# Attention scores with all products over 128 rows instead of 128 and 64 in turn

## The chip, the cores and the metric

The kernel runs on one core of one Trainium2 chip. The metric is the device time of one execution in microseconds (us); lower is better. Engines are named as the profile names them: PE is TensorE's matmul side, PEld its weight loads, DVE is VectorE, ACT is ScalarE, POOL is GpSimd, and SP is SyncE, which issues every DMA of this kernel.

## The reference, cut to what matters

Two transformer layers over 512 main tokens and 256 context tokens, width 1024. Layer 0 mixes a multi-scale pooling with grouped-query attention (12 query heads, 4 key heads, head size 64), layer 1 mixes a latent attention (8 heads of 64 + 32 = 96 dimensions) with a neighbourhood attention (8 heads of 64, each query against a window of 256 keys and 256 context keys). Each layer ends in a gated feed forward. Cut to the attention:

```
# layer 0: main tokens against 768 keys, context tokens against 256
s = einsum("bqhgd,bkhd->bhgqk", q, k) * 64 ** -0.5
o = einsum("bhgqk,bkhd->bqhgd", softmax(s), v)
# layer 1, latent heads, q and k of 96 dimensions: main tokens against 768 keys
# layer 1, neighbourhood heads
s_win = einsum("bqhd,bqkhd->bhqk", q_r, k_w) * scale + bias
s_ctx = einsum("bqhd,bchd->bhqc", q_r, k_ctx) * scale
p = softmax(concatenate([s_win, s_ctx]))
```

All of it is float32.

## The kernel before

Every float32 matrix is kept as two parts, H + L, each representable in the format fp32r that PE multiplies. An ordinary product (`mm3`, lines 134 to 138) is three matmuls: H with H, H with L and L with H.

For heads of 64 dimensions the parts of two heads, A and B, are stacked on the 128 partitions, so that two matmuls do. `stack_q` (line 345) writes QA = [A.H; A.L] and QB = [B.L; B.H]. `stack_k` (line 351) writes KA = [A.H; A.H], KB = [B.H; B.H] and KL = [A.L; B.L]; lines 356 and 357 are the two ACT copies that fill the second halves of KA and KB. A score block is then one product over 128 rows, Q with KA or KB, and one over 64 rows, the H half of Q with its half of KL (`hr = slice(64 * hd, 64 * hd + 64)`):

```
for ko in (MAIN, CTX):
    pe.matmul(S[:, ko], Q[:, tq], K[:, ko], start=True, stop=False)
    last = pe.matmul(S[:, ko], Q[hr, tq], KL[kp][hr, ko], start=False, stop=True)
```

The two kinds alternate in three places. Layer 0, main tokens (`main_units`, lines 767 and 768): 48 sets (6 pairs, 4 query tiles, 2 heads) of four products, of 512, 512, 256 and 256 keys. Layer 0, context tokens (`ctx_units`, lines 795 and 796): 12 sets of four products of 256. Layer 1, neighbourhood (`na_units`, lines 1057 and 1058): 16 units (4 pairs, 4 query blocks), each of two heads with four products of 256. The latent heads (`mla_units`) use `mm3` over 96 rows: 32 sets of six products, 512 three times and 256 three times, with no 64-row product among them.

All four loops run through `pipeline` (line 383). A unit is the scores and the softmax of one set: DVE takes the maximum (line 364), ACT the exponential (line 369), DVE a reciprocal (371), POOL the division (373). Two or three units later PE transposes the probabilities (line 380), ACT or DVE copies them out of PSUM (`copy_out`, lines 166 and 168), and PE multiplies them with the values (lines 746, 1026, 1206), each product with 64 columns of weights. Layer 0 also fits in steps of the modulation weights (line 206) whose loads come through the four buffers `wr`. Scores lie in two PSUM tiles `ps_big` or four `ps_one`.

The order of the instructions on each engine's queue, SP's too, is fixed when the program is built: a list scheduler walks the program in priority order on simulated times, so later work moves ahead where it is ready. Buffers come from pools; a tile waits until all readers of what lay in its place are done. The 12 slots `x3` (`slot3`) hold KA, KB and KL of the neighbourhood heads, later the latent keys; the slots `cH` and `cL` (8 each) hold the context's normalised input, later the biases. Before the neighbourhood loop six DMAs move halves of V into V2 (lines 1009, 1010), and each pair loads six bias tiles (1042), which POOL multiplies (1043). `turn_pair` (line 1096) transposes and splits latent queries and keys into rows 0 to 95 of their tiles. The tile `rows` (line 707) holds ten gain rows on all partitions for the whole run.

Of the kernel before, what the change touches and what calls it, by code (L numbers as in the profile page):

```python
# [26 lines left out]
# first 128-column tile of every 512-column block of layer 0's modulation weights, in the order of use  # L27
# [14 lines left out]
def trunk(ctx: ExitStack, tc: tile.TileContext, A: dict, out: bass.AP):  # L42
# [3 lines left out]
    # ------------------------------------------------------------------ pools  # L46
# [7 lines left out]
    def banks(i):  # L54
        """The 4 banks of PSUM that the next phase takes in pairs (ps_big) or one by one (ps_one)."""
        nonlocal ps
        psum.close()
        ps = psum.enter_context(tc.tile_pool(name=f"ps{i}", bufs=2, space=bass.MemoryType.PSUM))
# [19 lines left out]
    def group_pair(g, name):  # L78
        """H and L tiles for the main (g = 0: 512) or the context tokens (g = 1: 256)."""
        n, w = ((TM, "m"), (TC, "c"))[g]  # L80
        return tuple(base.tile([P, n], F32R, tag=w + x, name=name + x, bufs=KT) for x in "HL")
# [10 lines left out]
    # ---------------------------------------------------------------- loading  # L92
# [21 lines left out]

    def load(src, cols):
        raw = wrp.tile([P, 1024], F32, tag="wr", name="wraw")
        sp.dma_start(out=raw[:, :cols], in_=src)
        return raw

    def split(raw, cols, hp, tag="ws", bufs=3, eng=dve):  # L120
        """raw = H + L exactly, both representable in float32r."""
# [20 lines left out]
    def later(f, n=2):  # L142
        """Run f after the next n blocks of products have been issued."""
        waiting.append((blocks[0] + n, f))
        waiting.sort(key=lambda w: w[0])
# [6 lines left out]
    def run_chunks(chunks):  # L152
        """chunks: (load, compute(units)); loads run one chunk ahead."""
# [8 lines left out]
    def copy_out(dst, src, acts=1, of=2):  # L162
        """PSUM -> SBUF, `acts` of every `of` calls on the scalar engine."""
# [6 lines left out]
    # ------------------------------------------------------------ modulation  # L170
# [8 lines left out]
    def ada_quarter(qt, psum, ws, sbm, between=lambda: None):  # L179
        """shift and scale columns of feature tiles 2 qt, 2 qt + 1; ws: their weights [128, 512] per k tile"""  # L180
# [15 lines left out]
    def ada_steps(blocks, psum, slot):  # L196
        """Closures for column blocks (1024 wide) of layer 0's modulation: one per k tile, and a last one."""
# [54 lines left out]
    def square_sum(xs, sl, slot=lambda name: slot3(F32, name)):  # L252
        """sums of the squares over the k tiles"""
# [11 lines left out]
    def rstd_of(xs, sl, slot=lambda name: slot3(F32, name), between=lambda: None):  # L265
        """1 / rms of every token of the slice, on all partitions, in PSUM."""
# [29 lines left out]
    # ---------------------------------------------------------------- shared  # L296
    def tok_gemm(pt, units, kper, n, hs, ks=None):
        """pt [128 tokens, n] = h @ w over the k tiles (all, or ks of them); hs: per k (H, L) of the 128 tokens."""
# [5 lines left out]
    def tile_of(h, t):  # L304
        """per k (H, L) of token tile t (0-3 main, 4-5 context)."""
# [3 lines left out]
    def feature_gemm(pt, units, hs):  # L309
        """pt [128 features, tokens] over all k tiles; units: per k (WH, WL); hs: per k (H, L)."""  # L310
# [6 lines left out]
    def rope(dst, src, C, S, half, tmp):  # L317
        """dst = src * C + swap_halves(src) * S, over views [.., 2 * half]; the sum is left to later."""
# [5 lines left out]
    def head_rstd(view, sb, sqb=2):  # L324
        """1 / rms over the last axis of view [128, tiles, heads, d]; also the scratch tile for that."""
# [10 lines left out]
    def split_out(H, L, s, g=None):  # L336
        """PSUM s, times the column g if given -> H + L"""
# [7 lines left out]
    def stack_q(QA, QB, sl, s, g=None):  # L345
        """s [128: head A, head B] (times g) -> QA = [A.H; A.L], QB = [B.L; B.H] stacked on the partitions."""
# [4 lines left out]
    def stack_k(KA, KB, KL, sl, s, g=None):  # L351
        """KA = [A.H; A.H], KB = [B.H; B.H], KL = [A.L; B.L]."""
# [6 lines left out]
    # -------------------------------------------------------------- attention  # L359
    def softmax(S, nh, n, scale, pr, mx=None):  # L360
        """S [128 queries, nh heads, n keys] in PSUM -> normalised pr[head] [128, n] in SBUF."""
# [13 lines left out]
    def transposed(blocks, dst, acts=1, of=2):  # L375
        """128 x 128 blocks of probabilities -> dst [128 keys, len(blocks), 128 queries]."""
# [6 lines left out]
    def pipeline(units, fill, lag):  # L383
        """units: (scores + softmax, transposes) closures; fill: rates of background closures per step."""
# [26 lines left out]
    # ----------------------------------------------------------- feed forward  # L411
    def ffn(layer, xs, groups, chunks, last, background=None, grouped=None, ends=None, lead=1, pre=None, nbuf=(2, 1)):
        """Residual feed forward. groups: (token slice, condition, h); last(m) or, by the token groups `ends`, grouped(i).
        The first `lead` column tiles are taken group by group."""
        off, last_of = 0, []
        nmax = max(n for _, n in chunks)
        with ExitStack() as own:
# [4 lines left out]
            def ws_unit(src, cols):  # L422
                """weights, in turn in the buffers of the pool `pre` and of the one here"""
# [78 lines left out]
    def mix_out(layer, mixs, xs, groups, wp, after, ws):  # L502
        """groups: (token slice, condition, per k (H, L)); ws: the weights of the first output tiles."""
# [11 lines left out]
    # ================================================================ layer 0  # L515
# [32 lines left out]
    with tc.tile_pool(name="g0", bufs=1, side="left") as gp, tc.tile_pool(name="ws0", bufs=1, side="right") as wp:  # L548
# [5 lines left out]
        def pair_rows(kind, hv, t0, sink):  # L554
            """hv [128, token tiles from t0, 4 heads, 64]: RMS norm, rotation (main tokens), transposes: sink(pair, tokens, psum)."""
# [87 lines left out]
        # queries: pair p holds heads p (rows 0-63) and p + 6 (rows 64-127)  # L643
# [10 lines left out]
        def to_k(pr, *a):  # L654
            stack_k(KA[pr], KB[pr], KL[pr], *a)

        def first_chunk(units):
            """keys and the first queries, over the k tiles in quarters as their modulation comes in"""
# [48 lines left out]
        rows = base.tile([P, A["rows"].shape[1]], F32, tag="rows", name="rows")  # L707
        sp.dma_start(out=rows, in_=A["rows"].partition_broadcast(P))
        grow = {k: rows[:, a:b] for k, (a, b) in ROWCOLS.items()}
        # rotary tables with the head gains folded in  # L710
# [10 lines left out]
        KL = [kvp.tile([P, TT], F32R, tag=f"KL{i}", name=f"KL{i}") for i in range(2)]  # L721
# [10 lines left out]
    with tc.tile_pool(name="at0", bufs=1, side="left") as ap:  # L732
        pvq = []
        adaq = [f for b in (2, 4) for f in ada_steps([b, b + 1], ps_pv, lambda: m_slot("L", "adat"))]

        def pv_steps(p, t, last, k0, pts, st, m):
            """values of query tile t of a pair, two key tiles a step"""
# [15 lines left out]
        def main_units(p):  # L753
            pvs = {}
            kp = p // 3
            for t in range(4):
                pts = []
                for hd in range(2):
                    tq = slice(128 * t, 128 * t + 128)
                    hr = slice(64 * hd, 64 * hd + 64)  # L760
                    Q, K = (QA, QB)[hd][p], (KA, KB)[hd][kp]
                    st = {}

                    def scores(Q=Q, K=K, tq=tq, hr=hr, hd=hd, st=st):
                        S = ps_big([P, 1024])
                        for ko in (MAIN, CTX):
                            pe.matmul(S[:, ko], Q[:, tq], K[:, ko], start=True, stop=False)  # L767
                            last = pe.matmul(S[:, ko], Q[hr, tq], KL[kp][hr, ko], start=False, stop=True)  # L768
# [14 lines left out]
        def ctx_units(p):  # L783
            pvs = {}
            kp = p // 3
            for t in range(2):
# [3 lines left out]
                def scores(tq=tq, st=st):  # L790
                    S = ps_big([P, 2, 512])
                    for hd in range(2):
                        hr = slice(64 * hd, 64 * hd + 64)
                        Q, K = (QA, QB)[hd][p], (KA, KB)[hd][kp]
                        pe.matmul(S[:, hd, :TC], Q[:, tq], K[:, CTX], start=True, stop=False)
                        last = pe.matmul(S[:, hd, :TC], Q[hr, tq], KL[kp][hr, CTX], start=False, stop=True)
# [46 lines left out]
    class Ada1:  # L843
        """Layer 1's modulation goes along with layer 0's feed forward, on the vector engine."""
# [44 lines left out]
    # ================================================================ layer 1  # L889
# [534 lines left out]
```

## Time and profile before

| | |
|---|---|
| time, median of 3 runs | 1822.68 us (1812.99 to 1824.0) |
| span of the profiled execution | 1820.5 us, first to last instruction |
| what lies around the span | not listed apart; the median lies 2.2 us above it |
| PE busy | 1766.2 us (97%) |
| DVE, ACT, POOL busy | 947.5, 648.6, 234.4 us |
| mean granted TensorE clock | 0.978 |

PE's busy time is a union of modelled instruction spans, which overlap: the next matmul starts well before the one before it is shown to end. What a product costs is therefore read from start to start in the timeline, not from its shown length. The granted clock is 1.0 at 2.4 GHz and 0.5 at 1.2 GHz.

### The profile page before, as it was taken

The numbers are of one execution on the slowest core, as the hardware profiler recorded it, in microseconds if no ns is written. First come the engines' busy times: TensorE is split into PE (matmuls) and PEld (weight loads), VectorE is DVE, ScalarE is ACT, GpSimd is POOL, SyncE is SP. The second block draws the span as 40 slices with busy tenths as digits, with TensorE's granted clock in tenths as the row PEclk, the third lists the DMA queues.
The fourth block names the chain that finished last, engine by engine and source line by source line (L and its number), as shares of the span: only waits on it lengthen the run. The fifth ranks groups of instructions, "written<-read, shape, count | busy, mean of one in ns | idle before, by whom it ended". The sixth has DMA issues, their size and how long they took to land.

```text
span 1820.5 us, 28940 instructions
## 1 busy us (share of the span) xinstructions
PE 1766.2 (97%) x11590; PEld 1505.8 (83%) x11590; DVE 947.5 (52%) x2080; ACT 648.6 (36%) x1269; POOL 234.4 (13%) x360
## 2 busy tenths in 40 slices
PE   6899999999999999999999999998899999999999
PEld 3697556679888888888889999667778999899897
DVE  5686445545774533532336884446855543333332
ACT  4454334534321221121123563344455343232231
POOL 1342222301000000000000202323321000000000
PEclk9998999999999999999999999789999999999999
DMA  8310213421353532531222221102001222232221
GB/s 300 125 47 34 93 71 115 163 93 47 108 173 129 176 104 88 177 101 58 70 70 73 82 74 58 52 8 79 24 24 63 78 94 93 96 96 96 95 79 61
DMA packets 57638, 166.90 MB, mean 92 GB/s; under 512 B 6560, under 2 KB 13472, under 8 KB 57504
## 3 DMA queue, kind: packets, MB, share of 16 engines
q1 hardware_dynamic: 57504, 165.06, 27.3%
q8 instruction: 91, 1.49, 0.3%
q14 instruction: 43, 0.35, 0.1%
HBM read 160.05 MB, written 4.19 MB: 90 GB/s over the span
## 4 chain that ended last, share of the span: by engine, by line
PE 92%; DVE 4%; ACT 2%; DMA 1%; issue 1%; SPq 0%; POOL 0%; ACTq 0%; DVEq 0%; POOLq 0%
PE ps_one L137 16%; PE ps_one L138 16%; PE ps_one L136 16%; PE ps_tp L380 5%; PE ps_tp L138 5%; PE ps_tp L136 5%; PE ps_tp L137 5%; PE ps_pv L746 3%; PE ps_pv L1206 2%; PE ps_big L768 2%; PE ps_big L136 2%; PE ps_pv L1026 2%; PE ps_big L767 2%; PE ps_big L137 2%; PE ps_big L138 2%; PE ps_pv L136 1%
## 5 line engine op out<-in xcount | busy, mean ns | idle before, releaser
L124 ACT CAST wH<-wraw 128x1024 fp32r<-128x1024 f32 (+5 forms) x209 | 194.2, 937 | 382.9 <-PE ps_one L137 199.4
L125 DVE TENSOR_TENSOR wL<-wraw,wH 128x1024 fp32r<-128x1024 f32 (+4 forms) x199 | 222.5, 1122 | 171.2 <-ACT wH L124 168.7
L137 PE MATMUL ps_one<-hL,wH 128*128 128x512 f32 (+1 forms) x704 | 236.8, 336 | 0.0
L138 PE MATMUL ps_one<-hH,wL 128*128 128x512 f32 (+1 forms) x704 | 236.8, 336 | 0.0
L136 PE MATMUL ps_one<-hH,wH 128*128 128x512 f32 (+1 forms) x704 | 236.7, 336 | 0.0
L138 PE MATMUL ps_tp<-hH,wL 128*128 128x256 f32 x704 | 196.6, 280 | 0.0
L137 PE MATMUL ps_tp<-hL,wH 128*128 128x256 f32 x704 | 196.3, 279 | 0.0
L136 PE MATMUL ps_tp<-hH,wH 128*128 128x256 f32 x704 | 196.0, 280 | 0.0
L138 PE MATMUL ps_one<-aH,wL 128*128 128x512 f32 (+1 forms) x560 | 194.0, 347 | 0.0
L137 PE MATMUL ps_one<-aL,wH 128*128 128x512 f32 (+1 forms) x560 | 193.9, 347 | 0.0
L136 PE MATMUL ps_one<-aH,wH 128*128 128x512 f32 (+1 forms) x560 | 193.5, 347 | 0.0
L138 PEld LDWEIGHTS ps_one<-hH,wL 128*128 128x128 f32 x704 | 132.2, 188 | 15.4
L137 PEld LDWEIGHTS ps_one<-hL,wH 128*128 128x128 f32 x704 | 132.2, 188 | 14.5
L136 PEld LDWEIGHTS ps_one<-hH,wH 128*128 128x128 f32 x704 | 132.3, 188 | 14.1
L373 POOL TENSOR_SCALAR prob<-prob,rs 128x768 f32<-128x768 f32 (+2 forms) x136 | 106.0, 782 | 291.6 <-DVE rs L371 124.2
L290 POOL TENSOR_SCALAR hH<-nt 128x256 fp32r<-128x256 f32 (+1 forms) x72 | 39.5, 557 | 739.4 <-ACT nt L289 737.6
L136 PEld LDWEIGHTS ps_tp<-hH,wH 128*128 128x128 f32 x704 | 132.3, 188 | 0.9
L137 PEld LDWEIGHTS ps_tp<-hL,wH 128*128 128x128 f32 x704 | 132.0, 188 | 1.0
L138 PEld LDWEIGHTS ps_tp<-hH,wL 128*128 128x128 f32 x704 | 132.3, 188 | 0.1
L364 DVE TENSOR_REDUCE mx<-ps_big 128x1 f32<-128x768 f32 (+1 forms) x92 | 84.8, 922 | 90.9 <-PE ps_big L768 59.8
L136 PEld LDWEIGHTS ps_one<-aH,wH 128*128 128x128 f32 x560 | 105.8, 189 | 14.7
L137 PEld LDWEIGHTS ps_one<-aL,wH 128*128 128x128 f32 x560 | 105.6, 189 | 14.5
(297 smaller groups left out, 3623.1 us busy)
## 6 DMA issues: line engine op xcount, KB each, us to landing
wraw<-in_ada_dram SPq DMA_DIRECT2D x80, 512.0 KB, 3.9
wraw<-in_wg_dram SPq DMA_DIRECT2D x44, 512.0 KB, 3.5
wraw<-in_wu_dram SPq DMA_DIRECT2D x44, 512.0 KB, 3.5
wraw<-in_wd_dram SPq DMA_DIRECT2D x32, 384.0 KB, 3.1
wraw<-in_wd_dram SPq DMA_DIRECT2D x16, 512.0 KB, 3.5
wraw<-in_w1n_dram SPq DMA_DIRECT2D x12, 512.0 KB, 3.5
adaw<-in_adaq_dram SPq DMA_DIRECT2D x16, 256.0 KB, 5.4
wraw<-in_adaq_dram SPq DMA_DIRECT2D x8, 512.0 KB, 4.9
```

Source lines behind the costliest of these rows:

```text
L124: act.copy(H, raw[:, :cols])
L125: eng.tensor_tensor(L, raw[:, :cols], H.bitcast(F32), op=ALU.subtract)
L136: pe.matmul(o, aH, bH, start=first, stop=False)
L137: pe.matmul(o, aH, bL, start=False, stop=False)
L138: return pe.matmul(o, aL, bH, start=False, stop=last)
L290: last = (pool.tensor_scalar(H, t[:, :n], 1.0, 1.0, op0=ALU.mult, op1=ALU.mult), sub(L, t[:, :n], H))
L364: dve.reduce_max(mx[:, :nh], S, axis=AX)
L373: pool.tensor_scalar(pr[i], pr[i], r[:, i:i + 1], 1.0, op0=ALU.mult, op1=ALU.mult)
L380: pe.transpose(tp[:, 128 * i:128 * i + 128], b, ident)
L746: pe.matmul(st["pv"][64 * hd:64 * hd + 64, tq], V[kt][:, 64 * kv:64 * kv + 64], pts[hd][:, kt - k0, :], start=kt == k0, stop=kt == 5)
L767: pe.matmul(S[:, ko], Q[:, tq], K[:, ko], start=True, stop=False)
L768: last = pe.matmul(S[:, ko], Q[hr, tq], KL[kp][hr, ko], start=False, stop=True)
```

## The change

Layer 0: the low parts of the keys go into LA = [A.L; B.L] (the old KL). At the start of the attention a new function copies each half to both halves by DMA, so that LA = [A.L; A.L] and LB = [B.L; B.L], and the second product becomes Q, all 128 rows, with LA or LB. (It now also adds low times low.) This is done for both key pairs, for main and context columns apart: 12 DMAs. LB takes a new tile of the attention's pool and a slot `cH`.

Layer 1, neighbourhood: the roles turn round. Keys are stacked [A.H; A.L] and [B.L; B.H] by `stack_q` (no KL, no ACT copies), queries are split whole into QQ = (H, L), each [A; B], and at the start of each pair the same function copies halves: 6 DMAs a pair, 24 in all, into tiles with two buffers per part. V2 moves to three of the slots `x3` that KL held.

Latent heads: POOL sets rows 96 to 127 of each query and key tile to zero in `turn_pair` (80 memsets of 32 x 256), and the products run over 128 rows.

The tile `rows` is replaced by two loads of parts of it, four rows for layer 0 and, at the start of layer 1, six for layer 1. All else in the diff is comments taken out.

```diff
+    def gain_rows(hp, names):
+        at, end = ROWCOLS[names[0]][0], ROWCOLS[names[-1]][1]
+        rows = hp.tile([P, end - at], F32, tag="rows", name="rows")
+        sp.dma_start(out=rows, in_=A["rows"][:, at:end].partition_broadcast(P))
+        return {k: rows[:, ROWCOLS[k][0] - at:ROWCOLS[k][1] - at] for k in names}
...
+    def both_halves(XA, XB):
+        a, b = (x.bitcast(F32) for x in (XA, XB))
+        for hr in (slice(0, 64), slice(64, 128)):
+            sp.dma_start(out=b[hr], in_=a[64:128])
+        sp.dma_start(out=a[64:128], in_=a[0:64])
...
-            stack_k(KA[pr], KB[pr], KL[pr], *a)
+            stack_k(KA[pr], KB[pr], LA[pr], *a)
...
     with tc.tile_pool(name="at0", bufs=1, side="left") as ap:
+        LB = []
+        for a in LA:
+            LB.append((ap.tile([P, TM], F32R, tag="LB", name="LBm", bufs=2),
+                       base.tile([P, TC], F32R, tag="cH", name="LBc", bufs=KT)))
+            for b, ko in zip(LB[-1], GROUPS):
+                both_halves(a[:, ko], b)
+        LA = [tuple(a[:, ko] for ko in GROUPS) for a in LA]
...
-                    hr = slice(64 * hd, 64 * hd + 64)
-                    Q, K = (QA, QB)[hd][p], (KA, KB)[hd][kp]
+                    Q, K, L = (QA, QB)[hd][p], (KA, KB)[hd][kp], (LA, LB)[hd][kp]
...
-                        for ko in (MAIN, CTX):
+                        for g, ko in enumerate(GROUPS):
                             pe.matmul(S[:, ko], Q[:, tq], K[:, ko], start=True, stop=False)
-                            last = pe.matmul(S[:, ko], Q[hr, tq], KL[kp][hr, ko], start=False, stop=True)
+                            last = pe.matmul(S[:, ko], Q[:, tq], L[g], start=False, stop=True)
...
-                        last = pe.matmul(S[:, hd, :TC], Q[hr, tq], KL[kp][hr, CTX], start=False, stop=True)
+                        last = pe.matmul(S[:, hd, :TC], Q[:, tq], L[1], start=False, stop=True)
...
+    grow = gain_rows(lp, ("mqr", "mqrp", "mkr", "mkrp", "qag", "kvag"))
...
+    QQ = [[nap.tile([P, TM], F32R, tag=f"nQ{x}{i}", name=f"nQ{x}{i}") for x in "HL"] for i in range(4)]
...
-    KL = [slot3(F32R, name="nKL") for _ in range(4)]
...
-        to_q = lambda pr, *a: stack_q(QA[pr], QB[pr], *a)
-        to_k = lambda pr, *a: stack_k(KA[pr], KB[pr], KL[pr], *a)
+        to_q = lambda pr, sl, *a: split_out(QQ[pr][0][:, sl], QQ[pr][1][:, sl], *a)
+        to_k = lambda pr, *a: stack_q(KA[pr], KB[pr], *a)
...
-        V2 = [ap.tile([P, 512], F32, tag=f"V2{i}", name=f"V2{i}") for i in range(3)]
+        V2 = [slot3(F32, name=f"V2{i}")[:, :512] for i in range(3)]
...
+            QB = [ap.tile([P, TM], F32R, tag="nQB" + x, name="nQB" + x, bufs=2) for x in "HL"]
+            for a, b in zip(QQ[pr], QB):
+                both_halves(a, b)
...
-                            pe.matmul(S[:, so], Q[:, tq], K[:, ko], start=True, stop=False)
-                            last = pe.matmul(S[:, so], Q[hr, tq], KL[pr][hr, ko], start=False, stop=True)
+                            pe.matmul(S[:, so], QH[:, tq], K[:, ko], start=True, stop=False)
+                            last = pe.matmul(S[:, so], QL[:, tq], K[:, ko], start=False, stop=True)
...
+            for x in dst[2 * h2 + a]:
+                pool.memset(x[96:128, sl].bitcast(F32), 0.0)
...
-                            last = mm3(S[:, ko], (QH[:96, tq], QL[:96, tq]), (KH[:96, ko], KL_[:96, ko]), True, True)
+                            last = mm3(S[:, ko], (QH[:, tq], QL[:, tq]), (KH[:, ko], KL_[:, ko]), True, True)
```

## Rows read from the trace of the kernel before

**Rows 1.** The chain that ended last, shares of the span by engine.

```profile
PE 92%; DVE 4%; ACT 2%; DMA 1%; issue 1%; SPq 0%; POOL 0%; ACTq 0%; DVEq 0%; POOLq 0%
```

**Rows 2.** Stretches: length, each engine's busy us (instructions), clock, DMA share, GB/s.

```profile
188.50:334.90 146.40, 146.10 (x991) 88.35 (x990) 71.89 (x176) 60.24 (x130) 36.23 (x40) 1.00 0.27 98
1149.30:1168.10 18.80, 18.76 (x58) 12.50 (x58) 7.90 (x34) 7.07 (x19) 6.03 (x10) 0.50 0.11 32
1168.10:1212.50 44.40, 44.40 (x269) 30.14 (x270) 24.57 (x96) 19.98 (x50) 14.71 (x23) 1.00 0.07 20
1212.50:1229.50 17.00, 17.00 (x84) 12.12 (x82) 6.23 (x30) 6.53 (x16) 3.82 (x6) 0.70 0.00 0
```

**Rows 3.** Timeline, layer 0's output projection: two plain 128-row products of 512 in a row.

```profile
400.40 0.39 PE L138 MATMUL ps_one<-mixH,wL 128*128 128x512 f32 x1
...
400.63 0.40 PE L136 MATMUL ps_one<-mixH,wH 128*128 128x512 f32 x1
```

**Rows 4.** Timeline, one layer-0 main set: start us, us, engine, line.

```profile
188.84 0.47 PE L767 MATMUL ps_big<-KA,QA 128*128 128x512 f32 x1
...
189.25 0.18 PEld L768 LDWEIGHTS ps_big<-KL,QA 64*128 64x128 f32 x1 [0.24 <-issue]
189.25 0.49 PE L768 MATMUL ps_big<-KL,QA 64*128 64x512 f32 x1
...
189.67 0.38 PE L767 MATMUL ps_big<-KA,QA 128*128 128x256 f32 x1
...
189.99 0.38 PE L768 MATMUL ps_big<-KL,QA 64*128 64x256 f32 x1
...
190.29 0.66 PE L746 MATMUL ps_pv<-PT,V 128*64 128x128 f32 x8
```

**Rows 5.** Timeline, one latent set of six products, behind transposes, then values.

```profile
1348.21 0.48 PE L136 MATMUL ps_big<-mKH,mQH 96*128 96x512 f32 x1
...
1348.29 0.19 PEld L137 LDWEIGHTS ps_big<-mKL,mQH 96*128 96x128 f32 x1
1348.53 0.39 PE L137 MATMUL ps_big<-mKL,mQH 96*128 96x512 f32 x1
...
1348.99 0.28 PE L136 MATMUL ps_big<-mKH,mQH 96*128 96x256 f32 x1
...
1349.22 0.28 PE L138 MATMUL ps_big<-mKH,mQL 96*128 96x256 f32 x1
...
1349.43 0.54 PE L1206 MATMUL ps_pv<-PT,mV 128*64 128x128 f32 x3
```

**Rows 6.** Timeline, one context set of layer 0: its start and what follows.

```profile
338.95 0.36 PE L795 MATMUL ps_big<-KA,QA 128*128 128x256 f32 x1
...
340.18 0.66 PE L746 MATMUL ps_pv<-PT,V 128*64 128x128 f32 x8
```

**Rows 7.** Timeline, neighbourhood: eight products in a row, then transposes.

```profile
1209.18 0.38 PE L1057 MATMUL ps_one<-nKA,nQA 128*128 128x256 f32 x1
...
1211.69 0.66 PE L380 MATMUL ps_tp<-ident,prob 128*128 128x128 f32 x4
```

**Rows 8.** Timeline, neighbourhood: PE goes on behind its first wait.

```profile
1149.34 0.58 PE L1057 MATMUL ps_one<-nKA,nQA 128*128 128x256 f32 x1 [2.73 <-ACT prob L369]
1149.85 0.58 PE L1058 MATMUL ps_one<-nKL,nQA 64*128 64x256 f32 x1
```

**Rows 9.** Timeline of PE and ACT: layer 0's first score product, first exponential.

```profile
140.06 0.47 PE L767 MATMUL ps_big<-KA,QA 128*128 128x512 f32 x1 [1.56 <-DVE qn L560]
...
169.92 0.90 ACT L369 ACTIVATE prob<-ps_big,nb 128x768 f32<-128x768 f32 x1
```

**Rows 10.** DMA issues: KB each, median us from issue to landing.

```profile
wraw<-in_w1q_dram SPq DMA_DIRECT2D x4, 384.0 KB, 4.2
...
V<-mV SPq DMA_DIRECT2D x6, 128.0 KB, 2.3
```

**Rows 11.** Groups by line and shape, POOL: the nearest memset.

```profile
L172 POOL MEMSET cs<- 128x256 f32 x1 | 0.3, 315 | 0.0
```

More of the change, by code (lines that the diff above doesn't have):

```diff
@@ L706, in trunk @@
         sp.dma_start(out=pw, in_=A["pw"])
-        rows = base.tile([P, A["rows"].shape[1]], F32, tag="rows", name="rows")
-        sp.dma_start(out=rows, in_=A["rows"].partition_broadcast(P))
-        grow = {k: rows[:, a:b] for k, (a, b) in ROWCOLS.items()}
+        grow = gain_rows(gp, ("qg0", "qgp0", "kg0", "kgp0"))
         r0 = gp.tile([P, 2, 4, 64], F32, tag="rope0", name="rope0")
@@ L720, in trunk @@
         KB = [kvp.tile([P, TT], F32R, tag=f"KB{i}", name=f"KB{i}") for i in range(2)]
-        KL = [kvp.tile([P, TT], F32R, tag=f"KL{i}", name=f"KL{i}") for i in range(2)]
+        LA = [kvp.tile([P, TT], F32R, tag=f"KL{i}", name=f"LA{i}") for i in range(2)]
         mxp = [[mpp.tile([P, TT], F32R, tag=f"mp{i}{j}", name=f"mp{i}{j}") for j in range(2)] for i in range(2)]
@@ L759, in main_units, with scores @@
                     tq = slice(128 * t, 128 * t + 128)
-                    hr = slice(64 * hd, 64 * hd + 64)
-                    Q, K = (QA, QB)[hd][p], (KA, KB)[hd][kp]
+                    Q, K, L = (QA, QB)[hd][p], (KA, KB)[hd][kp], (LA, LB)[hd][kp]
                     st = {}
-                    def scores(Q=Q, K=K, tq=tq, hr=hr, hd=hd, st=st):
+                    def scores(Q=Q, K=K, L=L, tq=tq, hd=hd, st=st):
                         S = ps_big([P, 1024])
-                        for ko in (MAIN, CTX):
+                        for g, ko in enumerate(GROUPS):
                             pe.matmul(S[:, ko], Q[:, tq], K[:, ko], start=True, stop=False)
-                            last = pe.matmul(S[:, ko], Q[hr, tq], KL[kp][hr, ko], start=False, stop=True)
+                            last = pe.matmul(S[:, ko], Q[:, tq], L[g], start=False, stop=True)
                         st["p"] = ap.tile([P, 1, TT], F32, tag="P", name="prob", bufs=4)
@@ L792, in scores @@
                     for hd in range(2):
-                        hr = slice(64 * hd, 64 * hd + 64)
-                        Q, K = (QA, QB)[hd][p], (KA, KB)[hd][kp]
+                        Q, K, L = (QA, QB)[hd][p], (KA, KB)[hd][kp], (LA, LB)[hd][kp]
                         pe.matmul(S[:, hd, :TC], Q[:, tq], K[:, CTX], start=True, stop=False)
-                        last = pe.matmul(S[:, hd, :TC], Q[hr, tq], KL[kp][hr, CTX], start=False, stop=True)
+                        last = pe.matmul(S[:, hd, :TC], Q[:, tq], L[1], start=False, stop=True)
                     st["p"] = ap.tile([P, 2, TC], F32, tag="P", name="prob", bufs=4)
@@ L911, in trunk @@
     nap = na.enter_context(tc.tile_pool(name="na", bufs=1, side="left"))
-    QA = [nap.tile([P, TM], F32R, tag=f"nQA{i}", name=f"nQA{i}") for i in range(4)]
-    QB = [nap.tile([P, TM], F32R, tag=f"nQB{i}", name=f"nQB{i}") for i in range(4)]
+    QQ = [[nap.tile([P, TM], F32R, tag=f"nQ{x}{i}", name=f"nQ{x}{i}") for x in "HL"] for i in range(4)]
     V = [mV[t] for t in range(6)]
@@ L1053, in scores @@
                         S = ps_one([P, 512])
-                        Q, K = (QA, QB)[hd][pr], (KA, KB)[hd][pr]
-                        hr = slice(64 * hd, 64 * hd + 64)
+                        (QH, QL), K = (QQ[pr], QB)[hd], (KA, KB)[hd][pr]
                         for so, ko in ((slice(0, 256), wk), (slice(256, 512), CTX)):
-                            pe.matmul(S[:, so], Q[:, tq], K[:, ko], start=True, stop=False)
-                            last = pe.matmul(S[:, so], Q[hr, tq], KL[pr][hr, ko], start=False, stop=True)
+                            pe.matmul(S[:, so], QH[:, tq], K[:, ko], start=True, stop=False)
+                            last = pe.matmul(S[:, so], QL[:, tq], K[:, ko], start=False, stop=True)
                         mc = small.tile([P, 2], F32, tag="mc", name="mc")
```

## The prediction

> **What bounds the kernel now.** I read the chain that ended last first: it runs through PE for 92% of the span [rows 1]. Then the stretches, to see whether that holds where the change works: in layer 0's main attention PE is busy 146.1 of 146.4 us, DVE 71.9, ACT 60.2, POOL 36.2; in the steady part of the neighbourhood loop PE is busy all 44.4 us, DVE 24.6 [rows 2]. So the softmax engines wait for PE, and what PE saves there should come off the end. But a busy PE is not one at its peak, so I went to the timeline and measured from start to start.
>
> There the cost shows. Two plain 128-row products of 512 columns start 0.23 us apart [rows 3]. In a layer-0 score set, where 128 and 64 rows alternate, the steps are 0.41 and 0.42 us for 512 columns, 0.32 and 0.30 us for 256 [rows 4]. The weight load of the 64-row product starts together with its matmul, at 189.25 us, not ahead of it: PE finishes one kind before it loads the other. The latent sets are a control inside the same kernel: same loop, same neighbours, 96 rows throughout. Their second load starts 0.08 us after the first matmul, 0.24 us ahead of its own, and the steps are 0.23 us for 512 and (0.23 over two) 0.115 us for 256 [rows 5]. The first step behind the transposes is 0.32, the last one before the value products, which use 64 columns, 0.21: these two ends have a change of shape of their own and stay.
>
> **Part 1, the score products.** A main set now takes 188.84 to 190.29, 1.45 us [rows 4]. From the latent steps it will take 0.32 + 0.23 + 0.115 + 0.21 = 0.875 [rows 5], so 0.575 less; 48 sets give 27.6 us. A context set takes 1.23 us [rows 6]. Its first step, scaled from the latent one by its excess of 0.09, is 0.205; 0.205 + 0.115 + 0.115 + 0.21 = 0.645, so 0.585 less; 12 sets give 7.0 us. In the neighbourhood loop eight products in a row take 2.51 us up to the transposes [rows 7]; they will take about 0.205 + 7 x 0.115 = 1.01, so 1.5 less. Where a unit's two sets of four stand apart, each before values, it is 2 x 0.585 = 1.17. I take 1.33 for 14 units, 18.7 us. The first two units end in a wait of 2.73 us for ACT [rows 8], whose chain starts only when these scores are there; of their 3.0 us I take 1.0 and leave the rest to a longer wait. Three of the 14 units fall in the half-clock stretch, where the alternating step is 0.51 [rows 8] against 0.23 for a plain one (twice 0.115, an estimate): eight save 2.2 instead of 1.33, so 2.7 more. That makes 22.4.
>
> Does PE stay last? The main loop shrinks by at most the 27.6 us to 119: DVE is then at 61%, ACT at 51%. The steady neighbourhood stretch has 269 matmuls, at 8 scores, 8 transposes and 16 for the values a unit 8.4 units; less 8.4 x 1.33 it shrinks to 33 us: DVE at 74% [rows 2]. PE stays last, with less slack in a queue whose order is fixed; I take a tenth off here, 20 us. Sum: 27.6 + 7.0 + 20 = 54.6.
>
> **Part 2, the latent products.** From 96 to 128 rows: the 96-row step of 512 is 0.23 [rows 5], the 128-row one 0.23 too [rows 3]. No gain, no loss.
>
> **Part 3, the copies of halves.** The nearest DMA within the chip, 128 KB of V, lands in 2.3 us [rows 10]. The last of the three copies overwrites what the first two read, so a tile is ready after two landings; two tiles in turn make four, 9.2 us at most. SP stands still in between, and what is queued there is weight and bias loads. Layer 0: the first score product now runs at 140.06, but its exponential only at 169.92 [rows 9], so the chain has up to 29.9 us of cover even if the first sets move back; I cost it 0. With the cover gone it is 9.2. Neighbourhood: the first pair's queries are made long before the loop; from pair 2 on the buffers come free with the last scores of the pair before last, four units before they are wanted, each 44.4 / 8.4 - 1.33 = 4.0 us, so 16 us. Cover again, 7 us to spare; 0 taken, 9.2 a pair if not. The 24 ACT copies that go away cost PE nothing today; 0.
>
> **Part 4, the memsets.** 80 of 32 x 256 on POOL; the nearest row is 128 x 256 in 0.315 us [rows 11], so 25 us at most. They need only a free tile, so most can run in the neighbourhood loop, where POOL is busy 14.7 of 44.4 [rows 2]; those that come between POOL's pieces of the latent projections stand in a chain. 0 to 6 us, I take 1, being nearer to the idle POOL.
>
> **Part 5, the gain rows.** 384 KB less at the start, and as much more at the head of layer 1, where the nearest load of that size lands in 4.2 us [rows 10]. From -4.2 to 4.2; I take 0, since the same bytes move in both places and PE has weights on hand.
>
> **The clock.** In the neighbourhood loop the granted clock is 0.50 for 18.8 us behind the first wait, and 0.70 over 17.0 us although PE is busy in all of it [rows 2]; the second stretch starts right behind the alternating run that ends at 1211.69 [rows 7]. Layer 0's loop is at 1.00. With the products back to back the slow stretches may shorten: at best 18.8 x 0.5 + 17.0 x 0.3 = 14.5 us. If new waits lengthen them, they may double, 14.5 the other way. I take 1 us of gain, which cancels the memsets.
>
> So 54.6, rounded to 55. Made against the profiled span of 1820.5, it is 1765.5; the median of the runs shown lies 2.2 above that span, which gives **1768 us**.
>
> **The rivals.**
>
> A. Other queues take over. PE's order is fixed, and half the neighbourhood and context gain and a fifth of the main one turn into waits for DVE and ACT: 22.1 + 3.5 + 10 = 36, so 1787 us. For it: DVE at 74% and the 2.73 us wait. Against: almost all waits of the softmax end with PE today.
>
> B. The clock gives more: the slow stretches of the neighbourhood loop vanish, 1768 - 14 = 1754 us.
>
> C. The copies are exposed (slower than before). SP's order is fixed too; if the copies stand behind loads that wait for a buffer, scores wait for them, and PE, idle, falls to half clock behind each wait. Five places (layer 0 and four pairs), each 9.2 plus as much again as the first wait costs today, 18.8 x 0.5 = 9.4: 93 us against 54.6 saved, 1861 us. It decides from 11 us a place. Against it: SP's loads wait in layer 0 only once the loop has begun, and the cover above.
>
> D. The change does not do what it says: the steps stay long because the weight load stays in front of its matmul. Then nothing is saved, 1823 us. The trace speaks against it: in the latent set the load runs ahead although both products use the same rows [rows 5]. The Trainium skill speaks for it: its page TensorE: Matmul & The Clock Gate, section Part 3: Packing small matmuls — row/col tiling, says that a weight load overlaps a running matmul only when the row groups differ. By that rule every product of the new sets would show its load of about 0.19 us in front, and the sum would be 0; rows 5 disagree with it, for equal rows, so the chance stays small.
>
> **How the numbers follow.** Forecast 0.60, A 0.18, B 0.10, C 0.05, D 0.04, and 0.03 for other ends. The range reaches from B, less a little for the tenth taken off and the gain rows (1750), past A to 1800, where about half the sum would be eaten by exposed copies or memsets; C, D and some of the tails stay out. 1% is 18 us, about what a measurement of this kernel can tell from no change. Faster by more, under 1804: forecast, A, B, most of it, 0.88. Within: D and mixtures of A with part of C, 0.07. Slower: C, 0.05.
>
> **What would show it.** In the changed trace the products of one set should start 0.23 and 0.115 us apart with their loads ahead, and a main set should take 0.9 us; the main loop some 25 us less, the neighbourhood loop some 20. DVE's waits for scores should shrink, with PE still nearly full. The latent sets should be unchanged. Wrong would be: the first scores of a pair waiting for a copy, POOL's memsets ahead of the latent transposes, or steps still at 0.3 and 0.4 us.

## The result, and the profile after

The changed kernel takes 1769.84 us (median of 4 runs, 1769.16 to 1771.28) against 1819.41 for the kernel before beside it: ratio 0.9738, interval 0.9704 to 0.9771. The forecast was 1768. The profiled execution took 1770.36 us, span 1768.5. The total agrees with the forecast; most of its terms do not, and the table by stage shows it. Its last column is the best of the experiments below, the run `e9_layer0_early`. All stages are read from the timeline of one execution each, in us; the landmarks are the starts of first products and the ends of last ones. The forecast's 1 us for the clock has no row.

| stage | before | after | change | forecast | last run |
|---|---|---|---|---|---|
| start to first layer-0 score | 140.1 | 142.4 | +2.3 | 0 | 141.7 |
| to the first context score | 194.8 | 168.7 | -26.1 | -27.6 | 161.0 |
| to layer 0's last values | 46.2 | 39.2 | -7.0 | -7.0 | 39.3 |
| to the end of layer 0's feed forward | 617.2 | 617.2 | 0 | 0 | 617.2 |
| to the first neighbourhood score | 143.3 | 146.8 | +3.5 | 0 | 140.9 |
| to its last values | 98.8 | 68.9 | -29.9 | -20 | 66.8 |
| to the last latent values | 157.3 | 162.6 | +5.3 | +1 | 154.7 |

First the shape of a set. The timeline of the changed kernel, one layer-0 main set (PE is the product, PEld its weight load), against [rows 4]:

```profile
188.91 0.47 PE L786 MATMUL ps_big<-KA,QA 128*128 128x512 f32 x1
189.00 0.19 PEld L787 LDWEIGHTS ps_big<-LA,QA 128*128 128x128 f32 x1
...
189.23 0.40 PE L787 MATMUL ps_big<-LA,QA 128*128 128x512 f32 x1
...
189.46 0.28 PE L786 MATMUL ps_big<-KA,QA 128*128 128x256 f32 x1
...
189.58 0.28 PE L787 MATMUL ps_big<-LA,QA 128*128 128x256 f32 x1
...
189.79 0.34 PE L766 MATMUL ps_pv<-PT,V 128*64 128x128 f32 x2
```

The steps are 0.32, 0.23, 0.12 and 0.21 us, 0.88 in all: the four numbers that the prediction took from the latent set. The load of LA starts 0.09 us after the product ahead of it, on the same 128 rows. Then a context set, against [rows 6], and eight neighbourhood products, against [rows 7], in the same view:

```profile
318.84 0.36 PE L813 MATMUL ps_big<-KA,QA 128*128 128x256 f32 x1
...
319.49 0.66 PE L766 MATMUL ps_pv<-PT,V 128*64 128x128 f32 x8
...
1134.30 0.36 PE L1078 MATMUL ps_one<-nKA,nQH 128*128 128x256 f32 x1
...
1135.41 0.65 PE L1044 MATMUL ps_pv<-PT,mV 128*64 128x128 f32 x4
```

0.65 us (was 1.23) and 1.11 (was 2.51; where transposes follow, as in [rows 7], it is now 1.06). The stretches, against [rows 2]: layer 0's main loop in its steady part, the first and the steady part of the neighbourhood loop (length; busy PE, PEld, DVE, ACT, POOL; clock; DMA share; GB/s):

```profile
185.70:311.10 125.40, 124.49 (x1017) 87.29 (x1016) 74.39 (x182) 61.61 (x134) 38.67 (x43) 1.00 0.33 118
1109.40:1126.40 17.00, 8.13 (x37) 7.87 (x37) 6.60 (x31) 6.05 (x14) 3.88 (x8) 0.50 0.51 119
1126.40:1170.00 43.60, 43.60 (x368) 35.14 (x367) 30.53 (x133) 27.07 (x68) 23.98 (x49) 1.00 0.28 71
```

PE is still busy nearly throughout, DVE at 59% and 70%; there is no second slow stretch in the neighbourhood loop. But in the 17 us around its start, from 1109.40 on, PE is busy only 8.13. The chain that ended last, against [rows 1], gives the DMA 2% for 1%:

```profile
PE 91%; DVE 4%; DMA 2%; ACT 2%; issue 1%; POOL 1%; SPq 0%; ACTq 0%; POOLq 0%; DVEq 0%
```

Two places of the new kernel show why. The first is the head of the neighbourhood loop: timeline of SP's queue and of PE.

```profile
1102.13 0.47 SPq L1027 DMA_DIRECT2D V<-mV  x1
...
1107.24 0.46 SPq L370 DMA_DIRECT2D nQBH<-nQH  x1
...
1112.05 0.46 SPq L371 DMA_DIRECT2D nQH<-nQH  x1
...
1114.36 0.55 PE L1078 MATMUL ps_one<-nKA,nQH 128*128 128x256 f32 x1 [7.19 <-DMA nQH<-nQH]
...
1122.07 0.58 PE L1078 MATMUL ps_one<-nKA,nQH 128*128 128x256 f32 x1 [3.91 <-ACT prob L383]
```

The first pair's queries had been made long before. What the first half copy waits for is its target: `nQB` lies in the attention's pool, whose memory comes free with the last product of the projections. SP stands 3.3 us for that product, until the moment at which PE stops, 1107.2 (SP's waits):

```profile
SPq L370 <- PE ps_one L145: 3.3, 1, 3.3
```

The copies of V ahead of it, into slots `x3`, go off without that wait. In the kernel before V's copies went into that pool, and there it was they that stood for the same product:

```profile
SPq L1009 <- PE ps_one L138: 4.5, 1, 4.5
```

Behind the wait come two landings, one after the other, since the in-place copy can start only when the two before it have landed, and three more copies of V stand between the first half copy and the second (1107.79 to 1109.67): PE stands 7.19 us. The stage ahead of the loop is only 3.5 us longer all the same, because its projections end after 139.6 us instead of 143.3: ACT has 64.3 us of work there instead of 77.8, two of PE's waits (1.13 and 0.76 us) are gone, and so is a stretch of 3.4 us at half clock.

The second place is the head of layer 0's loop, timeline of SP, PE and ACT:

```profile
166.42 2.40 SPq L370 DMA_DIRECT2D LBm<-LA  x4
169.31 1.73 SPq L371 DMA_DIRECT2D LA<-LA  x2
...
172.78 0.50 PE L787 MATMUL ps_big<-LA,QA 128*128 128x512 f32 x1 [1.26 <-DMA LA<-LA]
...
176.95 0.90 ACT L383 ACTIVATE prob<-ps_big,nb 128x768 f32<-128x768 f32 x1
...
177.99 0.79 PE L786 MATMUL ps_big<-KA,QA 128*128 128x512 f32 x1 [4.49 <-ACT prob L383]
```

Here too SP had stood for the target's memory before it issued the copies of 166.42, last for transposes of the projections (SP's waits):

```profile
SPq L370 <- PE ps_tp L586: 2.9, 1, 2.9
```

Before, the first exponential ran at 169.92 [rows 9] and the wait ahead of the third set was 0.72 us:

```profile
177.39 0.49 PE L767 MATMUL ps_big<-KA,QA 128*128 128x512 f32 x1 [0.72 <-ACT prob L369]
```

Now the first two sets wait for LA and LB, the first exponential comes 7 us later, both score buffers are held, and PE stands.

### The profile page after: what moved, and what is told of

It reads as the page before. It is cut to its first block, busy times and chain, and to the rows that moved or that the text cites. A ratio compares the mean times of both kernels' runs of the same rounds, so it can differ in the third digit from the quotient of the medians.

```text
span 1768.5 us, 29065 instructions
## 1 busy us (share of the span) xinstructions
PE 1695.4 (96%) x11590; PEld 1482.4 (84%) x11590; DVE 945.3 (53%) x2072; ACT 634.4 (36%) x1237; POOL 253.3 (14%) x440
## 4 chain that ended last, share of the span: by engine, by line
PE 91%; DVE 4%; DMA 2%; ACT 2%; issue 1%; POOL 1%; SPq 0%; ACTq 0%; POOLq 0%; DVEq 0%
PE ps_one L144 17%; PE ps_one L143 17%; PE ps_one L145 17%; PE ps_tp L394 5%; PE ps_tp L145 5%; PE ps_tp L143 5%; PE ps_tp L144 5%; PE ps_pv L766 3%; PE ps_pv L1229 2%; PE ps_big L143 2%; PE ps_big L145 2%; PE ps_big L144 2%; PE ps_pv L1044 1%; PE ps_big L786 1%; PE ps_pv L143 1%; PE ps_pv L144 1%
## 5 line engine op out<-in xcount | busy, mean ns | idle before, releaser
L145 PEld LDWEIGHTS ps_one<-aH,wL 128*128 128x128 f32 x560 | 105.5, 188 | 14.5
```

The costliest lines, as they stand in the source:

```text
L145: return pe.matmul(o, aL, bH, start=False, stop=last)
```

## The experiments

Each was timed beside the kernel before on the same chip; ratios are to that.

### Is it the change of shape?

**Grouping, layer 0.** The kernel before, same products, other order:

```diff
                         for ko in (MAIN, CTX):
                             pe.matmul(S[:, ko], Q[:, tq], K[:, ko], start=True, stop=False)
+                        for ko in (MAIN, CTX):
                             last = pe.matmul(S[:, ko], Q[hr, tq], KL[kp][hr, ko], start=False, stop=True)
```

(and in the context sets first both heads' 128-row products, then both heads' 64-row ones)

> The kernel before, with only the order of the products in layer 0's score sets changed: both 128-row products first, then both 64-row ones. Same instructions, same rows. Theory (each change between 128 and 64 rows costs about 0.19 us, the 64-row product itself nothing extra): two of the four changes of a main set go, 1.45 us becomes 0.23 + 0.30 + 0.23 + 0.30 = 1.06, 48 sets save 18 to 19 us; a context set 1.23 becomes 0.83 if going from rows 0-63 to rows 64-127 is no change, 1.03 if it is, 12 sets save 2.4 to 4.8. Together 1795 to 1799 us. Rival (a 64-row product is slow by itself, wherever it stands): steps and time unchanged, 1819 us. Rival D's rule (a load overlaps only where row groups differ): every product of a group shows its load, 1819 us or more.

Measured: 1795.06 us, 0.9872 (0.9825 to 0.9919). A grouped main set in the timeline (here transposes follow):

```profile
190.72 0.62 PE L767 MATMUL ps_big<-KB,QB 128*128 128x512 f32 x2
191.27 0.29 PEld L769 LDWEIGHTS ps_big<-KL,QB 64*128 64x128 f32 x2 [0.25 <-issue]
191.27 0.61 PE L769 MATMUL ps_big<-KL,QB 64*128 64x512 f32 x2
191.81 0.44 PE L380 MATMUL ps_tp<-ident,prob 128*128 128x128 f32 x2
```

Over the main sets the median is 1.460 us before, 1.071 grouped, 0.875 after; with three, one and no change of rows inside the set. (1.460 - 0.875) / 3 = 0.195, and 1.071 - 0.875 = 0.196: one price explains both. A 64-row product is not slow, a change is. Rival D falls: grouped products don't show their loads. The context sets are 0.73 us and hold something unexpected, in the grouped kernel's timeline:

```profile
320.43 0.37 PE L796 MATMUL ps_big<-KA,QA 128*128 128x256 f32 x1
320.64 0.28 PE L796 MATMUL ps_big<-KB,QB 128*128 128x256 f32 x1
320.85 0.38 PE L800 MATMUL ps_big<-KL,QA 64*128 64x256 f32 x1
320.85 0.38 PE L800 MATMUL ps_big<-KL,QB 64*128 64x256 f32 x1
321.16 0.34 PE L746 MATMUL ps_pv<-PT,V 128*64 128x128 f32 x2
```

The two 64-row products, rows 0-63 and 64-127, start together (0.003 us apart, median of 12 sets) and run side by side.

**Grouping, neighbourhood too**, by the order of the calls alone:

```diff
+                    Ss = [ps_one([P, 512]) for _ in range(2)]
+                    for so, ko in ((slice(0, 256), wk), (slice(256, 512), CTX)):
+                        for hd in range(2): ... 128-row product of head hd into Ss[hd][:, so]
+                        for hd in range(2): ... 64-row product of head hd into Ss[hd][:, so]
```

> The kernel before with grouping alone, now in the neighbourhood loop too: for the window's columns, then for the context's, both heads' 128-row products and then both heads' 64-row products, which lie on rows 0-63 and 64-127. No copies, no padding, no split gain rows. Theory (a change between 128 and 64 rows costs 0.19 us, and two 64-row products on opposite halves run side by side, as the context sets of the grouped run show with starts 0.003 us apart): a set of four takes 0.73 us as there, the eight products of a unit 1.46 instead of 2.51 us, 16 units save 15 to 17 us against the grouped run's 1795: 1778 to 1780 us, and down to 1772 if the half-clock stretches of that loop go as well. Rival (side by side holds only in the context sets, because they are followed by values): 0.115 more per pair and a change between the halves, 1.46 + 2 x 0.3 = 2.1 us a unit, 1788 us. The DMA copies of the change would then be worth more than grouping by over 20 us.

Measured: 1794.98 us, 0.9854 (0.9828 to 0.9880), no gain over layer 0 alone, and neither theory was tested. The timeline shows why:

```profile
1149.82 0.36 PE L1059 MATMUL ps_one<-nKA,nQA 128*128 128x256 f32 x1
1150.11 0.38 PE L1062 MATMUL ps_one<-nKL,nQA 64*128 64x256 f32 x1
1150.42 0.38 PE L1059 MATMUL ps_one<-nKA,nQA 128*128 128x256 f32 x1
```

What was written was not what stood in PE's queue: the products alternate as before, 0.31 us apart. So the order was held with `tc.issue_after`, each product behind the one written before it:

> The run before again, in which the trace showed that the neighbourhood products had been put back into alternation in PE's queue (only the first unit was grouped), so that nothing was tested there. Now each product is queued behind the one written before it. Theory and rival as there: with 0.73 us a set of four 1778 to 1780 us, 1772 if the half-clock stretches of that loop go; with pairs that do not run side by side 1788 us. A third outcome: the heads' two softmax chains now start together and later than the first one did, and PE waits for them: 1790 us or more.

Measured: 1778.59 us, 0.9782 (0.9750 to 0.9814), as the theory has it. One set of four in the timeline, with its two 64-row products side by side:

```profile
1155.43 0.39 PE L1067 MATMUL ps_one<-nKA,nQA 128*128 128x256 f32 x1
1155.65 0.28 PE L1067 MATMUL ps_one<-nKB,nQB 128*128 128x256 f32 x1
1155.86 0.38 PE L1070 MATMUL ps_one<-nKL,nQA 64*128 64x256 f32 x1
1155.87 0.38 PE L1070 MATMUL ps_one<-nKL,nQB 64*128 64x256 f32 x1
```

Units that run in one piece take 1.47 us before values (theory 1.46), and in all 32 pairs the two 64-row products start 0.003 to 0.004 us apart. From its first score to its last values the stage takes 76.2 us, 99.7 in the run that groups layer 0 alone; the score steps are 17.8 us of that, and the stretch at half clock late in the loop is not there. Without one copy, one memset or one more byte of buffers, the order of the products alone brings about 41 of the change's 50 us.

### Where the parts stand

**Layer 0 alone, neighbourhood alone, gain rows alone.** The first is the changed kernel with layer 1's products, copies and memsets as before; the second the kernel before with QQ, QB, `stack_q` and the neighbourhood products of the change; the third the kernel before with the two loads of gain rows.

```diff
 layer 0 alone, to the changed kernel (and the latent part at 96 rows without memsets):
-        to_k = lambda pr, *a: stack_q(KA[pr], KB[pr], *a)
+        to_k = lambda pr, *a: stack_k(KA[pr], KB[pr], KL[pr], *a)
-                            last = pe.matmul(S[:, so], QL[:, tq], K[:, ko], start=False, stop=True)
+                            last = pe.matmul(S[:, so], Q[hr, tq], KL[pr][hr, ko], start=False, stop=True)
...
 neighbourhood alone: the same lines of the kernel before, the other way round, and
+            QB = [ap.tile([P, TM], F32R, tag="nQB" + x, name="nQB" + x, bufs=2) for x in "HL"]
+            for a, b in zip(QQ[pr], QB):
+                both_halves(a, b)
...
 gain rows alone, to the kernel before:
+        grow = gain_rows(gp, ("qg0", "qgp0", "kg0", "kgp0"))
+    grow = gain_rows(lp, ("mqr", "mqrp", "mkr", "mkrp", "qag", "kvag"))
```

> The changed kernel with layer 1 as before (neighbourhood and latent products, their copies and memsets all as they were); the change only in layer 0's scores. Theory (parts are separate): 34.6 us by the prediction's two terms for layer 0, less about 2 for the later start of the first score seen in the changed kernel, so 32 us less than before, 1787 us. Rival (the later start of the neighbourhood stage after the change comes from layer 0): less than 30.

> The kernel before with the change only in the neighbourhood scores (their copies, and the copies of V in other slots). Theory (separate parts, the stage gains 30 us by shorter steps and by the clock, and starts 3.5 later): 26 us less than before, 1793 us, and no stretch at half clock between the second unit and the end of the stage. Rival (the clock is higher in the changed kernel because of what came before the stage): a slow stretch as in the kernel before, 18 to 20 us less, 1800 us.

> The kernel before with only the gain rows split into two loads, one at the start, one at the head of layer 1. Theory: no difference, 1819 us, first layer-0 score at 140.1 us. Rival (the split load is what moves the first score from 140.1 to 142.4 us, or what makes the neighbourhood stage start 3.5 us later): 2 to 4 us more.

Measured: 1785.55 us (0.9831, 0.9785 to 0.9876), 1790.63 (0.9862, 0.9808 to 0.9917) and 1816.44 (0.9998, 0.9974 to 1.0023). The kernel before took 1816.95 beside them, so the parts are worth 31.4, 26.3 and 0.5 us, close to their theories. The first has the split gain rows in it; with the memsets' 6.2 below taken off, the sum is 51.5. The medians differ by 49.6, the spans of the two profiles by 52.0: the parts are separate. The first layer-0 score came at 141.4 to 142.2 us in all three and in the grouped run, with and without the split rows, and at 140.2 in a run below that has them: the 2.3 us ahead of it are scatter between executions. The neighbourhood-only run starts its loop 146.7 us after the feed forward, so those 3.5 us belong to this part.

The third run has a lesson about the clock. It has the old neighbourhood products and yet no second slow stretch:

```profile
1170.20:1238.00 67.80, 67.80 (x453) 47.42 (x451) 33.05 (x129) 30.03 (x72) 19.55 (x30) 1.00 0.05 14
```

Its loop takes 94.0 us, the one before 98.8. The slow stretch at 1212 of [rows 2] is thus not a fixed cost of alternation: of the executions profiled with alternating products there, four have a stretch at 0.50 in the loop's later half and one has none; of the eight with 128 rows or held order none has one.

### What the copies and memsets cost

**Latent part as before**, without the memsets; and the memsets alone, with 96-row products:

```diff
-            for x in dst[2 * h2 + a]:
-                pool.memset(x[96:128, sl].bitcast(F32), 0.0)
...
-   mm3(S[:, ko], (QH[:, tq], QL[:, tq]), (KH[:, ko], KL_[:, ko]), True, True)
+   mm3(S[:, ko], (QH[:96, tq], QL[:96, tq]), (KH[:96, ko], KL_[:96, ko]), True, True)
```

> The changed kernel with the latent part as it was: no memsets of zeros, latent score products over 96 rows. Theory (the latent stage is 5.3 us longer after the change because the 80 memsets stand on POOL between its pieces of the latent projections): 4 to 5 us less than the changed kernel, about 1765 us, and the stretch from the last neighbourhood values to the first latent score is back near 38 us from 42. Rival (the 5.3 us are the clock, or the place where weights stand, and only the arrival at that stage has moved): no change, 1770 us.

> The changed kernel with its 80 memsets, but the latent score products over 96 rows as before. Theory (the memsets cost, the 32 more rows do not): 1770 us, as the changed kernel, and 4 to 5 us more than without memsets. Rival (the 128-row products cost): as without memsets.

Measured: 1763.6 us (0.9698, 0.9669 to 0.9727) and 1772.02 (0.9746, 0.9717 to 0.9774). The memsets cost 6.2 us against the changed kernel and 8.4 against the memsets-only run, more than expected; the 32 more rows cost nothing (the latent score steps sum to 39.2 us with 128 rows, 40.1 with 96). From the last neighbourhood values to the first latent score it is 42.4 us in the changed kernel, 41.8 with the memsets alone and 36.1 without them. Timeline of POOL in the changed kernel:

```profile
1183.79 2.34 POOL L1126 MEMSET mQH<- 32x256 f32 x9
...
1187.79 0.99 POOL L132 TENSOR_TENSOR wL<-wraw,wH 128x384 fp32r<-128x384 f32 x1
...
1195.01 0.31 POOL L1126 MEMSET mQH<- 32x256 f32 x1
1195.40 0.76 POOL L1143 TENSOR_TENSOR qr<-krr,rq 128x128 f32<-128x128 f32 x2
```

and without memsets:

```profile
1185.24 3.94 POOL L132 TENSOR_TENSOR wL<-wraw,wH 128x384 fp32r<-128x384 f32 x4 [9.34 <-ACT wH L131]
1192.06 0.76 POOL L1141 TENSOR_TENSOR qr<-krr,rq 128x128 f32<-128x128 f32 x2 [2.89 <-DVE rq L257]
```

The weights' low part and the rotated key part `qr` come 2.5 and 3.3 us earlier there, although the stage starts 0.8 later. Of the 80 memsets 35 had run when the neighbourhood loop ended; 45 stand in POOL's order behind it, many of them between those pieces. One costs 0.31 us, as much as the 128 x 256 one of [rows 11] with four times the rows.

**Earlier copies in the neighbourhood**, issued as soon as the queries are there, into slots that are free then (V2 goes back to the pool of the attention); then with the latent part as before:

```diff
+    QQB = [[slot3(F32R, name="nQB" + x)[:, :TM] for x in "HL"] for _ in range(2)]
...
                     latents("w1q", 384, 384, main, "qag", (cqH, cqL)),
+                    (lambda: None, lambda u: [both_halves(a, b) for pr in range(2) for a, b in zip(QQ[pr], QQB[pr])]),
```

> The changed kernel, with the half copies of the first two neighbourhood pairs issued behind the latent query projection, into slots that are free then, instead of behind the bias loads and the copies of V on SP. Theory (the 7.19 us in which PE stands before the first neighbourhood score are that queue, and a part of the half-clock stretch behind it goes as well): the wait falls under 2 us, the time by 5 to 8 us, to 1762 to 1765 us. Rival (the copies of V or the biases are there no earlier, so another wait stands in the same place; or the waits move to the weight loads that now stand behind the copies on SP): within 2 us of the changed kernel.

> Both edits together: latent part over 96 rows without memsets, and the early half copies. If they are separate, their gains add: 1757 to 1761 us. If the latent stage's loss came from the neighbourhood stage ahead of it, less.

Measured: 1760.48 us (0.9686, 0.9656 to 0.9715) and 1755.43 (0.9656, 0.9627 to 0.9685), both a little more gain than expected. The edit moves the order on SP and the target at once; SP's wait above says that it was the target that held the copy. V's copies, back in the attention's pool, stand 5.1 us for the last projection product here, and PE waits for none of them. The 7.19 us are gone; what is left is the chain of the first softmax:

```profile
1110.23 0.39 PE L1082 MATMUL ps_one<-nKA,nQH 128*128 128x256 f32 x1 [3.24 <-ACT prob L383]
```

The gain is 9.4 us for a wait of 7.19: the stretch at half clock there shrinks too, from 17.1 to 3.4 us.

**Earlier copies in layer 0**, on top of both edits: the 512-token part of the first group, into a buffer of its own (the second group's LBm goes into a free slot of another pool):

```diff
+        LB0 = kvp.tile([P, TM], F32R, tag="LB0", name="LBm")
...
+       (lambda: None, lambda u: both_halves(LA[0][:, MAIN], LB0))   # behind pooling(0)
```

> Both edits of the run before (early neighbourhood copies, latent part over 96 rows), and the 512-token half copies of layer 0's first group of heads issued behind the pooling chunk, into a buffer of their own, instead of behind the last projections. In the changed kernel PE stands 1.26 us in the first layer-0 score set for the copy of the upper half, and 4.49 us ahead of the next set for the first softmax. Theory (that second wait is long because the first set was held up by the copy; before the change it was 0.72 us): both waits together fall to about 1 us, 4 to 5 us less than without this edit, 1750 to 1752 us. Rival (PE then waits for the first softmax just as long, which starts when the 512-token projections leave ACT free): within 1 us, 1755 us.

Measured: 1746.13 us, 0.9606 (0.9581 to 0.9631), the best version: 9.3 us less, twice the expectation. The two waits without this edit, in the run with both earlier edits:

```profile
172.14 0.50 PE L787 MATMUL ps_big<-LA,QA 128*128 128x512 f32 x1 [1.74 <-DMA LA<-LA]
177.34 0.80 PE L786 MATMUL ps_big<-KA,QA 128*128 128x512 f32 x1 [4.48 <-ACT prob L383]
```

The timeline with it, SP, ACT, PE:

```profile
95.30 1.16 SPq L370 DMA_DIRECT2D LBm<-LA  x2
...
167.53 0.90 ACT L383 ACTIVATE prob<-ps_big,nb 128x768 f32<-128x768 f32 x1
...
173.26 0.55 PE L394 MATMUL ps_tp<-ident,prob 128*128 128x128 f32 x3 [0.85 <-DVE QB L350]
174.53 0.50 PE L788 MATMUL ps_big<-KA,QA 128*128 128x512 f32 x1 [0.72 <-ACT prob L383]
```

LA can be copied at 95.30; the changed kernel does it at 166.42, because LBm lay in a pool whose memory came free only then. The wait ahead of the third set is back at 0.72 us. The expectation counted the waits alone, and there it was right: all of PE's waits in layer 0's main loop fall from 7.8 to 2.9 us. The other 4.4 us lie beside the slow stretches that the run with both earlier edits has there (142.1 to 145.5 and 172.8 to 183.0 us) and this one has not. The profiles alone don't show that the edit removed them: three runs with the same grouped layer 0 have 0, 6.8 and 13.7 us at half clock in this loop and take 170.7, 173.2 and 176.3 us for it. But all five executions of the last run show a mean granted clock of 0.990 to 0.994, those without the edit 0.985 to 0.990.

## Why the prediction was right, and where it was not

The total came right by luck: two errors cancelled. Products and clock gave some 72 us, as the last run has it, where 55.6 were forecast, and the copies and memsets cost some 24 where the prediction had set 0 and 1. Two of its own three signs of being wrong came: the first scores of a pair waited for a copy, and memsets stood ahead of the latent transposes.

- **Part 1, sets.** Right in its mechanism and in its steps: 0.88, 0.65 and 1.06 us (1.11 before values) against 0.875, 0.645 and 1.01. Layer 0's score steps in the main sets sum to 72.1 us before and 41.6 in the last run, 30.5 less for 27.6; the medians make 28.1 of it, and the rest are sets that ran at half clock before. The context term was exact. The Trainium skill, TensorEngine Tiling (Array Packing), Key Properties, says that a change of tiling mode drains TensorE; the runs agree and price it, 0.19 us a change. The rule behind rival D does not hold here for equal rows: the load at 189.00 runs under the product before it.
- **Neighbourhood, 20 us forecast, 29.9 measured.** The gross 22.4 for the scores was right (their steps fall from 47.5 to 24.6 us). The tenth taken off was wrong: PE's one wait in the loop, for ACT, grew from 2.73 to 3.91 us, less than the 2.0 that the gross sum had allowed for it, and no other came up. And 6.9 us came from products that did not change: the transposes' steps fall from 19.4 to 17.7 us, the values' from 30.1 to 24.9, because less of their work is at half clock. Rival B had this; the forecast took 1 us. Of these 6.9 us, 4.7 are missing in the gain-rows run too (18.0 and 26.8 us), with the old products, so they need not be the change's.
- **Part 3, the failed step.** Both covers were judged by when the data is ready and when it is wanted, not by when the target's memory is free. In layer 0 the cover of 29.9 us did not count, since the pool of LBm, and so the issue, came at 166.42; in the neighbourhood the first pair's queries were ready, but the pool of `nQB` came free only with the last projection product, when PE was about to want the copies. From the second pair on the cover held. Rival C came nearest, at two of its five places. It priced a place at 9.2 us of copies and 9.4 of clock; measured were 9.4 us in all at one (a wait of 7.19) and 9.3 in all at the other (4.9 of waits). That these lie near its 9.2 is chance. The 24 ACT copies, set at 0 as well, are the likely reason why the projections ahead end 2.2 to 3.9 us earlier in every profile that has the new stacking; no run tested it alone.
- **Part 4.** Mis-sized: 6.2 us (8.4 by the other pair of runs) for 1, past the upper bound of 6. That "most can run in the neighbourhood loop" did not hold: 45 of 80 came behind it, many between POOL's pieces of the latent projections.
- **Parts 2 and 5** were right at 0.
- **The clock.** Between 130 and 1300 us the stretches at 0.50 sum to 61 us before, 38 after, 14 in the last run. They shrink with PE's waits; how much of it is scatter, as in the gain-rows run, stays open. The scatter is not small: the 47 executions of the kernel before beside the experiments take 1810 to 1825 us, and most of those under 1814 have a mean granted clock of 0.985 or 0.986, most of those over 1822 one of 0.977 to 0.979, while the changed kernel's four lie within 2.2 us. Against the former the change is worth some 42 us, not 50.

So products and clock are worth some 72 us (1818.1 to 1746.13 in the last run), and the three costs, 9.4, 9.3 and 5 to 6 us, leave the 49.6 that were measured, within 2 us.

## What to carry to other kernels

Look in start-to-start times for products that change shape in turn: equal rows, or the same products grouped, take the price away, and grouping needs no copies (but read the order in PE's queue, not in the source). Cost a copy by when its target's memory is free (both pools here came free only with the last readers of what lay there before) and by what stands around it in its queue, not by when its source is ready. A "free" filler on an idle engine costs what stands behind it there.

## What was not expected of the hardware

- Two 64-row products on opposite halves of the rows start 0.003 us apart and run side by side. The Trainium skill, TensorE: Matmul & The Clock Gate, Part 3: Packing small matmuls — row/col tiling, describes this with about 4 ns from start to start; the trace agrees.
- Two waits at the head of a stage cost more than their length: 9.4 us for 7.19, and 9.3 for 4.9, each time with a half-clock stretch beside it that went too. In the second case scatter may have a part in it.
- The slow stretch late in the neighbourhood loop came in four of five executions with the same alternating products. What decides it was not found.
